# Two pairs' attention values together in eleven blocks, an opening in another order, and norm_g loaded by partitions (fp16 three-pass attention block, one core)

## The chip, the cores and the metric

The kernel runs on one core of one Trainium2 chip. The metric is the device time of one execution in microseconds (us). Before the change the median of three runs is 1378.2 us (1378.13 to 1381.88).

## The reference

One layer is computed on x of shape (1, 4096, 1024) in float32:

```
xn = rms_norm(x, norm_g)
q, k, v, z = split(xn @ w_in)          # 16 query heads, 4 key/value heads of 64
s = q k^T / 8 + bias[t5_bucket(distance)]   # keys of the last 128 positions only
p = softmax(concat(s, sink of the head))    # the sink's column is dropped afterwards
o = p v
x = x + (o * silu(z)) @ w_out
out = rms_norm(x, final_g)
```

All in float32. The kernel gets x as it is and a second time transposed, and the weights with their columns in an order that suits it.

## The kernel before

**Numbers.** TensorE works in fp16. Each operand is split into a high and a low fp16 half, and each product is three passes (high x high, high x low, low x high; PASSES, L331) that add up in one PSUM bank. A split takes two instructions: ScalarE writes the high half, and VectorE subtracts it from the operand and writes the low half (L161 to 163). Operands that are sums go through GpSimd first.

**Blocks and products.** The 4096 tokens are worked off in 16 blocks of 256 (counted 0 to 15 here; the change's own words count from one, so its "blocks 5 to 15" are 4 to 14). The projections to q and z and the output projection are 2 x 2 block products. In the first two or three blocks they are done plainly, with eight half-products; from then on with seven products of sums and differences, in a chain over three PSUM banks. Weight factors that don't stay in SBUF are streamed from DRAM (tag "ws").

**Attention in pairs.** A block has four pairs (gp, t): gp is a half of the key/value heads, t a half of the block's tokens. A pair goes through these steps, most of them twice (e = 0, 1, one key/value head each, with its four query heads):
- scores (L567 to 580): eight matmuls into a PSUM bank "s" (two buffers)
- post (L583 to 608, VectorE): bias, window and maximum
- exps (L612 to 617, ScalarE): exponentials with their sums
- normalise (L620 to 625, VectorE): the reciprocal of the sum (L623), then one multiplication of a 128 x 512 tile in SBUF (L625), "the norm"
- turn (L627 to 645): four transposes on TensorE into a PSUM bank "tp" (L634, two buffers); ScalarE writes the high half from it (L638), VectorE the low half (L641) and a masked copy (L642)
- values (L647 to 661): twelve matmuls of 128 x 64 weights with 512 columns into the PSUM bank "o"; two of them run side by side, each on its half of the array's columns
- gate (L666 to 668, VectorE): the product with silu(z), out of "o"

PSUM has eight banks: "tp" twice, "s" twice, "o", and "pa", "pb", "pc" for the products. A bank "tp" serves one more thing: the factors of the next block's rms_norm are turned into a row there by two transposes (x_row, L297), with which VectorE scales the transposed x (x_scale, L302) before it is split (x_split, L309 and L311). The first block uses a "tp" for its bias rows as well.

**The order.** Every block is 25 slots (SLOTS), and each product or half-product stands in one slot. A dict (STEADY, L848) says for each step in which slot, counted from its block's first, it stands. In "pairs" the twelve numbers of a pair are: scores, post, exps, norm and turn of e = 0, the same five of e = 1, then values and gate. Steps after slot 24 run beside the next block's: "slot 39" of one block is "slot 14" of the next. Within a slot the steps are put out by phase (PHASES, L785), in this order: bank, attn (post, values, gate, x_row), sum, norm, turn, high, move (x_scale), low, soft (exponentials), load, main (the product), scores. From slot 90 of the whole kernel on (STATIC), TensorE, ScalarE, VectorE and GpSimd each run their instructions in just that order. In the first 20 slots only TensorE's order is set by hand, between the two the scheduler orders them. The opening (L998), ahead of slot 0, is by hand on all four. SyncE issues the loads.

**The opening.** The first key and value weights are loaded (L110) behind x, transposed x and norm_g (L115, from ScalarE's queue); each of their eight parts is scaled by norm_g and split (split_kv, L995). Beside that the first block's x is squared, its factors are computed (x_factor, L282 and L284), turned (L297), x is scaled and split. Then the first projection (L463) runs.

Of the kernel before, what the change touches and what calls it, by code (L numbers as in the profile page):

```python
# [10 lines left out]
F16 = mybir.dt.float16  # L11
# [10 lines left out]
P = 128  # L22
KC = D // P
TB = 256
NTB = T // TB
# [33 lines left out]
def tile_swa_block(ctx, tc, x, xt, t5, norm_g, final_g, w_q, w_kv, w_z, sinks, w_out, hot, out):  # L59
    nc = tc.nc  # L60
# [3 lines left out]
    work = ctx.enter_context(tc.tile_pool(name="work", bufs=1))  # L64
# [9 lines left out]
    def atile(shape, dt, tag, bufs):  # L74
        return pools["attn"].tile(shape, dt, tag=tag, name=tag, bufs=bufs)
# [5 lines left out]
    def ps(tag, bufs=1, shape=(P, 512), dt=F32):  # L81
        return psum.tile(list(shape), dt, tag=tag, name=tag, bufs=bufs)


    gs = const.tile([P, KC], F32, name="gs")
    mhalf = const.tile([P, 1], F32, name="mhalf")
    nc.vector.memset(mhalf, -0.5)
# [13 lines left out]
    def load_xf(tb):  # L101

        for i in range(2):
            xf[tb, i] = work.tile([P, 4, TB], F32, tag="xf", name="xf", bufs=2)
            nc.sync.dma_start(xf[tb, i], xt[tb, :, 4 * i:4 * i + 4, :])

    def load_kv(kc):
        st = work.tile([P, 512], F32, tag=("q00", "q01", "q10", "q11", "z00", "z01", "z10", "z11")[kc], name="wst",
                       bufs=1)
        nc.sync.dma_start(st, w_kv[kc * P:(kc + 1) * P, :])  # L110
        return st

    load_xin(0)
    load_xf(0)
    nc.scalar.dma_start(gs, norm_g.rearrange("(c p) -> p c", p=P))  # L115
    kv = [load_kv(kc) for kc in range(KC)]
    th = const.tile([BUCKETS, H], F32, name="th")
    nc.scalar.dma_start(th, t5)
# [42 lines left out]
    def split(hi, lo, f, scale):  # L161
        nc.scalar.activation(hi, f, AF.Copy, scale=scale)
        nc.vector.scalar_tensor_tensor(lo, f, scale, hi, op0=OP.mult, op1=OP.subtract)
# [6 lines left out]
    def load_pair(w, c, st):  # L170

        for j in range(2):
            nc.sync.dma_start(st[:, j, :], w[(4 * j + c) * P:(4 * j + c + 1) * P, :])
        return st
# [24 lines left out]
    def plain_q(name, c, st):  # L199
        w = wq[HOME[name]]  # L200
        split(w[:, c, 0], w[:, c, 1], factor(name, True, st), g_of(name, True, c))
# [73 lines left out]
    def x_square(tb, t):  # L275

        sq[tb, t] = work.tile([P, 1], F32, tag="rs", name="rs", bufs=2)
        nc.scalar.activation(xin[tb, t], xin[tb, t], AF.Square, accum_out=sq[tb, t])
# [8 lines left out]
    def x_factor(tb):  # L287
        for t in range(2):
            xs[tb, t] = power(sq.pop((tb, t)), 1.0 / (D * SX * SX), EPS / (SX * SX), "x")

    rows = {}

    def x_row(tb):

        p = ps("tp", 2)[:, 0:TB]
        for t in range(2):
            nc.tensor.transpose(p[:, t * P:(t + 1) * P], xs[tb, t].to_broadcast([P, P]), ident)  # L297
        rows[tb] = p

    def x_scale(tb, i):  # L300
        f = xf[tb, i]
        nc.vector.tensor_tensor(f, f, rows[tb][:, None, :].to_broadcast([P, 4, TB]), op=OP.mult)  # L302
# [3 lines left out]
    def x_split(tb, i):  # L306

        d = work.tile([P, 4, 2, TB], F16, tag=f"xb{i}", name="xb", bufs=1)
        nc.scalar.activation(d[:, :, 0, :], xf[tb, i], AF.Copy)  # L309
        XB[tb, i] = d  # L310
        return lambda: nc.vector.tensor_tensor(d[:, :, 1, :], xf[tb, i], d[:, :, 0, :], op=OP.subtract)  # L311
# [121 lines left out]
    def shift_k(tb):  # L433

        keys_of.clear()
        nc.vector.tensor_copy(K[:, :, :, :, 0:P], K[:, :, :, :, TB:])
# [82 lines left out]
    gf = const.tile([P, D], F32, name="gf")  # L519

    def bias_rows():
        pe = ps("tp", 2)
        nc.tensor.matmul(pe[:H, :2 * WIN], th, hb, start=True, stop=True)
        return pe

# [23 lines left out]
    class Pair:  # L549


        def __init__(self, tb, gp, t):
            self.tb, self.gp, self.t = tb, gp, t
            self.first = tb == 0 and t == 0
            self.s, self.pt, self.pm, self.c = {}, {}, {}, None
            self.steps = [0, 0]

# [69 lines left out]
        def turn(self, e):  # L627

            self.step(e, 3)
            p = ps("tp", 2)  # L630
            pv = p.rearrange("p (h q) -> p h q", h=4)
            for u in range(4):
                r, hp = divmod(u, 2)
                nc.tensor.transpose(pv[:, 2 * hp:2 * hp + 2, r * HD:(r + 1) * HD], self.c[:, 4 * e + u, :P], ident)  # L634
            w = atile([P, 2, 512], F16, f"pt{e}", 1)
            m = atile([P, 2, 512], F16, f"pm{e}", 1)
            self.pt[e], self.pm[e] = w, m
            nc.scalar.activation(w[:, 0], p, AF.Copy, scale=SP)  # L638

            def low():  # L640
                nc.vector.scalar_tensor_tensor(w[:, 1], p, SP, w[:, 0], op0=OP.mult, op1=OP.subtract)  # L641
                nc.vector.tensor_tensor(m.rearrange("p l (h q) -> p (l h) q", h=4),  # L642
                                        w.rearrange("p l (h q) -> p (l h) q", h=4),
                                        own_m[:, None, :].to_broadcast([P, 8, P]), op=OP.mult)
            return low

        def values(self):  # L647

            o = ps("o")
            tb, t = self.tb, self.t  # L650
            if self.first:
                todo = [(self.pm, V[tb], 0)]
            else:
                todo = [(self.pt, V[tb] if t else V[tb - 1], 1 - t), (self.pm, DV[tb], t)]
            n = 3 * len(todo)
            k = 0
            for w, v, vt in todo:
                for vi, pi in PASSES:
                    for e in range(2):
                        g = 2 * self.gp + e  # L660
                        nc.tensor.matmul(o[e * HD:(e + 1) * HD, :], v[:, vt, vi, g * HD:(g + 1) * HD], w[e][:, pi],  # L661
                                         start=k == 0, stop=k == n - 1)
                    k += 1
            self.o = o
# [176 lines left out]
    def plain_t(slots, tb, key, names, left, place, done):  # L841
# [25 lines left out]
    }  # L867
    SHORT = (1, 2, 2, 4, 6, 2, 3, 3, 5, 7, 8, 9)

    def moved(pairs, by):  # L870
        return {p: tuple(s + d for s in v) for (p, v), d in zip(pairs.items(), by)}
# [7 lines left out]
    LAST = dict(STEADY, vd=LAST_V, dv=LAST_DV, zs12=LAST_Z12, zp22=LAST_ZP, zs22=LAST_Z22,  # L879
                pairs={p: tuple(s + d for d in SHORT) for p, s in zip(STEADY["pairs"], LAST_PAIRS)},  # L880
                oplain=LAST_O, yplain=dict(zip(BLOCKS, LAST_Y)), res=25)
# [2 lines left out]
    PLAIN_X = dict(xsplit=(21, 22), xsum={"t1": 22, "t2": 24, "t3": 26, "t4": 27},  # L884
                   xsumsplit={"t1": 23, "t2": 25, "t3": 29, "t4": 28})

    NEXT_TO_LAST = dict(STEADY, op=(49, 48, 47, 51), on=(50, 54), om=(51, 55), os=(52, 56))

    def block(tb):
        s0 = SLOTS * tb  # L890
        plan = {0: FIRST, NTB - 2: NEXT_TO_LAST, NTB - 1: LAST}.get(tb, STEADY)

# [5 lines left out]
        isplain = {n: tb < m for n, m in PLAIN.items()}  # L898
        last = tb == NTB - 1
        isplain["o"] |= last  # L900
        if tb in PAIRS_BY:
            plan = dict(plan, pairs=moved(plan["pairs"], PAIRS_BY[tb]))
        if isplain["z"]:
            plan = dict(plan, **PLAIN_X)
# [84 lines left out]
    for tb in range(NTB):  # L989
        block(tb)  # L990
# [4 lines left out]
    def split_kv(kc):  # L995
        split(wkv[:, kc, 0], wkv[:, kc, 1], kv[kc], gs[:, kc:kc + 1])

    def opening():  # L998
        shift_k(0)
        for t in range(2):  # L1000
            x_square(0, t)
        x_factor(0)
        split_kv(0)
        x_row(0)
        for i in range(2):
            x_scale(0, i)
        low = x_split(0, 0)
        split_kv(1)
        low()
        low = x_split(0, 1)  # L1010
        split_kv(2)
        low()
        rows = bias_rows()
        for kc in range(3, KC):
            split_kv(kc)
        first_kv()
        spread = make_bias(rows)
        for c in range(4):
            st = (work.tile([P, 2, D], F32, tag="ws", name="wst", bufs=4) if c < 3 else
                  ramp.tile([P, 2, D], F32, tag="raw3", name="wst", bufs=1))  # L1020
            raw["q", c] = load_pair(w_q, c, st)
        spread()
        for c in range(3):
            raw["z", c] = load_pair(w_z, c, ramp.tile([P, 2, D], F32, tag=f"raw{c}", name="wst", bufs=1))
        for name in BLOCKS[:2]:
            for c in range(4):
                plain_q(name, c, raw["q", c])
        low_k, low_v = evac_k(0, banks["k", 0]), evac_v(0, banks["v", 0])
        low_k()
        low_v()  # L1030
        for name in BLOCKS[2:]:
            for c in range(4):
                plain_q(name, c, raw["q", c])

    ENGINES = {mybir.EngineType.PE, mybir.EngineType.Activation, mybir.EngineType.DVE, mybir.EngineType.Pool}
    with tc.manual_schedule(engines=ENGINES):
        opening()
# [68 lines left out]
```

## Time and profile before

| | |
|---|---|
| median of three runs | 1378.2 us |
| profiled execution | 1378.95 us, span 1377.2 us |
| TensorE matmuls busy | 1338.4 us (97% of the span), granted clock 0.994 |
| VectorE busy | 1203.0 us (87%) |
| ScalarE busy | 799.8 us (58%) |
| GpSimd busy | 439.5 us (32%) |
| DMA | 381.65 MB, mean 277 GB/s |

The profile is one execution, recorded by the hardware profiler. PE is TensorE's matmuls, PEld its weight loads, DVE VectorE, ACT ScalarE, POOL GpSimd, SP SyncE. A row of a timeline gives the start in us, the duration in us, the engine, the line of the kernel, the operation and its tiles (out<-in); in brackets stands the idle time ahead of it and what ended it. A row of busy times by stretch gives the stretch, its length, then each engine's busy time with its count of instructions, the granted TensorE clock (1.00 is full speed), the busy share of the DMA engines and what they moved in GB/s. Matmuls are pipelined and their records overlap, so their own durations don't add up; distances from start to start do.

### The profile page before, as it was taken

The numbers are of one execution on the slowest core, as the hardware profiler recorded it, in microseconds if no ns is written. First come the engines' busy times: TensorE is split into PE (matmuls) and PEld (weight loads), VectorE is DVE, ScalarE is ACT, GpSimd is POOL, SyncE is SP. The second block draws the span as 40 slices with busy tenths as digits, with TensorE's granted clock in tenths as the row PEclk, the third lists the DMA queues.
The fourth block names the chain that finished last, engine by engine and source line by source line (L and its number), as shares of the span: only waits on it lengthen the run. The fifth ranks groups of instructions, "written<-read, shape, count | busy, mean of one in ns | idle before, by whom it ended". The sixth has DMA issues, their size and how long they took to land.

```text
span 1377.2 us, 39296 instructions
## 1 busy us (share of the span) xinstructions
PE 1338.4 (97%) x16246; PEld 1086.0 (79%) x16246; DVE 1203.0 (87%) x2719; ACT 799.8 (58%) x2052; POOL 439.5 (32%) x406
## 2 busy tenths in 40 slices
PE   5899999999999999999999999999999999999997
PEld 4898678687697888869788796978879697887963
DVE  6989898888879889898988989899898989989795
ACT  5767565655555665565565555566556555555562
POOL 0612333524324142341513224242322414333121
PEclk9899999999999999999999999999999999999999
DMA  9995996889978495876949677694966769486576
GB/s 356 316 386 216 342 388 225 335 325 345 353 264 333 175 340 192 288 268 231 346 148 334 225 267 265 235 339 150 336 243 242 285 219 337 166 323 225 198 266 260
DMA packets 75603, 381.65 MB, mean 277 GB/s; under 512 B 9472, under 2 KB 10784, under 8 KB 42912
## 3 DMA queue, kind: packets, MB, share of 16 engines
q1 hardware_dynamic: 64352, 358.12, 71.2%
q10 hardware_dynamic: 11072, 21.02, 4.1%
q8 instruction: 127, 2.08, 0.6%
q14 instruction: 52, 0.43, 0.1%
HBM read 340.05 MB, written 39.06 MB: 275 GB/s over the span
## 4 chain that ended last, share of the span: by engine, by line
PE 79%; DVE 10%; DMA 5%; issue 2%; ACT 2%; POOL 0%; SPq 0%; ACTq 0%; POOLq 0%; DVEq 0%
PE pa L375 16%; PE pb L375 16%; PE pc L704 10%; PE o L661 6%; PE pc L375 5%; PE s L580 5%; PE pb L394 5%; PE pc L473 5%; PE pa L704 5%; PE tp L634 3%; PE pb L704 3%; DVE wsp L239 2%; DMA wst<-in_wq 1%; DMA wst<-in_wz 1%; DVE c L608 1%
## 5 line engine op out<-in xcount | busy, mean ns | idle before, releaser
L375 PEld LDWEIGHTS <-ws 128*128 128x128 f16 x7008 | 401.1, 98 | 25.7 <-issue 14.1
L704 PEld LDWEIGHTS <-yo 128*128 128x128 f16 x1392 | 134.0, 98 | 145.5 <-issue 3.6
L375 PEld LDWEIGHTS <-wq 128*128 128x128 f16 x3984 | 227.1, 98 | 11.9 <-issue 6.5
L617 ACT ACTIVATE c<-c,m 128x129 f32<-128x129 f32 x512 | 199.2, 392 | 28.3 <-DVE m L608 27.6
L704 PE MATMUL pc<-ws,yo 128*128 128x512 f16 x744 | 170.4, 379 | 0.2 <-DMA ws<-wos 0.2
L608 DVE CUSTOM_DVE_ANT_0 c<-s,bias,sink 128x128 f32<-128x128 f32 x496 | 153.6, 348 | 7.3
L284 POOL TENSOR_TENSOR rr<-ms,mhalf 128x1 f32<-128x1 f32 x62 | 36.1, 589 | 343.2 <-DVE ms L282 275.7
L625 DVE TENSOR_TENSOR c<-c,rl 128x512 f32<-128x512 f32 x128 | 130.8, 1024 | 3.8
L641 DVE SCALAR_TENSOR_TENSOR pt<-tp,pt 128x512 f16<-128x512 f32 x128 | 87.2, 684 | 36.9 <-ACT pt L638 36.8
L375 PE MATMUL pb<-xs,ws 128*128 128x128 f16 x1872 | 111.2, 220 | 0.0
L322 POOL TENSOR_TENSOR xf<-xf 128x512 f32<-128x512 f32 x56 | 83.3, 1497 | 86.8 <-DVE xb L311 72.6
L580 PE MATMUL s<-K,q 128*128 128x192 f16 x1024 | 108.5, 247 | 2.1 <-DVE m L608 2.0
L698 DVE TENSOR_TENSOR yo<-y,yo 128x512 f16<-128x512 f32 x100 | 81.6, 816 | 32.5 <-ACT yo L697 32.5
L404 ACT ACTIVATE mc<-pa 128x512 f32<-128x512 f32 x67 | 39.9, 595 | 118.6 <-PE pa L375 92.5
L375 PE MATMUL pb<-xb,ws 128*128 128x128 f16 x1776 | 107.3, 221 | 0.0
L404 ACT ACTIVATE mc<-pb 128x512 f32<-128x512 f32 x53 | 31.6, 596 | 125.5 <-PE pb L375 93.2
L690 POOL TENSOR_TENSOR y<-y,y 128x512 f32<-128x512 f32 x48 | 75.7, 1576 | 88.4 <-DVE y L668 45.1
L642 DVE TENSOR_TENSOR pm<-pt,own_m 128x1024 f16<-128x1024 f16 x128 | 96.4, 755 | 3.7
L580 PEld LDWEIGHTS <-q 128*128 128x128 f16 x1024 | 86.2, 98 | 14.9 <-DVE m L608 3.6
L617 ACT ACTIVATION_READ_ACCUMULATOR c<-c,m 128x1 f32 x512 | 96.7, 189 | 0.0
L187 POOL TENSOR_TENSOR wst<-wst 128x512 f32<-128x512 f32 x48 | 71.1, 1491 | 79.4 <-ACT wst L225 45.6
L638 ACT ACTIVATE pt<-tp 128x512 f16<-128x512 f32 x128 | 74.1, 594 | 36.5 <-PE tp L634 28.7
(135 smaller groups left out, 2680.2 us busy)
## 6 DMA issues: line engine op xcount, KB each, us to landing
ws<-wos SPq DMA_DIRECT2D x68, 1024.0 KB, 5.4
ws<-wzss SPq DMA_DIRECT2D x52, 1024.0 KB, 5.5
ws<-wost SPq DMA_DIRECT2D x48, 1024.0 KB, 5.3
ws<-wzs SPq DMA_DIRECT2D x47, 1024.0 KB, 5.5
ws<-wqs SPq DMA_DIRECT2D x31, 1024.0 KB, 5.0
xin<-in_x SPq DMA_DIRECT2D x34, 512.0 KB, 4.3
xf<-in_xt SPq DMA_DIRECT2D x32, 512.0 KB, 4.4
r<-in_x SPq DMA_DIRECT2D x30, 512.0 KB, 5.3
```

The costliest lines, as they stand in the source:

```text
L322: nc.gpsimd.tensor_tensor(dst, l, r, op=OP.subtract)
L375: nc.tensor.matmul(place(p, c), left(kc, wi)[:, c * P:(c + 1) * P], right_x(tb, right, kc, xi), start=fresh and c == 0 and k == 0, stop=c ...
L580: nc.tensor.matmul(s[:, hp, 0:3 * HD], lhs, rhs, start=hl == 0, stop=hl == 1)
L608: nc.vector.tensor_tensor_reduce(out=cu, in0=sv, in1=b, scale=-1.0 / SCORE, scalar=sink[:, g, r, hp:hp + 1], op0=OP.add, op1=OP.min, accum ...
L617: nc.scalar.activation(cu, cu, AF.Exp, bias=self.m[:, u:u + 1], scale=-1.0, accum_out=self.l[:, u:u + 1])
L625: nc.vector.tensor_tensor(cu, cu, rl[:, :, None].to_broadcast([P, 4, P]), op=OP.mult)
L641: nc.vector.scalar_tensor_tensor(w[:, 1], p, SP, w[:, 0], op0=OP.mult, op1=OP.subtract)
L642: nc.vector.tensor_tensor(m.rearrange("p l (h q) -> p (l h) q", h=4), w.rearrange("p l (h q) -> p (l h) q", h=4), own_m[:, None, :].to_bro ...
L661: nc.tensor.matmul(o[e * HD:(e + 1) * HD, :], v[:, vt, vi, g * HD:(g + 1) * HD], w[e][:, pi], start=k == 0, stop=k == n - 1)
L690: nc.gpsimd.tensor_tensor(Y[(tb, *dst)], Y[(tb, *l)], Y[(tb, *r)], op=op)
L698: return lambda: nc.vector.tensor_tensor(yo[:, 1], s, yo[:, 0], op=OP.subtract)
L704: nc.tensor.matmul(p, YO[tb, left][:, yi, c * P:(c + 1) * P], right(c, wi), start=fresh and k == 0, stop=k == 11, skip_group_check=not fresh)
```

## The change

Four things are changed.
- In blocks 4 to 14 (MERGED) the values of pairs (0,t) and (1,t) stand in the same slot, 29 and 39, one after the other, and their gates in slots 30 and 40 (BY_TWO). Before, the four values stood in slots 25, 29, 36 and 39, the gates in 27, 31, 38 and 40. With that, the turn of (1,0), e = 1, goes from slot 26 to 25, that of (0,1), e = 1, from 32 to 31, and pair (1,1)'s two turns, both in slot 37 before, to slots 38 and 36, and its two norms, both in slot 35 before, to slots 35 and 34. The next block's row of factors goes from slot 13 to 14, and its scaling from slot 14 to 15.
- The two "tp" buffers become two banks "tp" and "tq". In the merged blocks the second pair's values go into "tq", and all turns and the row use "tp" alone; elsewhere turns alternate between the two (turn_bank). The second pair's turned tiles come out of buffers "wsp" and "op".
- In the opening, the first split of the key weights stands behind the row and the scaling of block 0's x.
- norm_g is handed over in the shape of its tile, (128, 8), and loaded as it lies in DRAM; before, it lay as 1024 numbers in a row and the load picked them one by one.

```
+    def turn_bank(tb):
+        turns.append(0)
+        return ps("tp" if MERGED <= tb < NTB - 1 or len(turns) % 2 else "tq")
...
-    nc.scalar.dma_start(gs, norm_g.rearrange("(c p) -> p c", p=P))
+    nc.scalar.dma_start(gs, norm_g)
...
-        p = ps("tp", 2)[:, 0:TB]
+        p = turn_bank(tb)[:, 0:TB]
...
+            self.second = MERGED <= tb < NTB - 1 and gp == 1
...
-            p = ps("tp", 2)
+            p = turn_bank(self.tb)
...
-            w = atile([P, 2, 512], F16, f"pt{e}", 1)
-            m = atile([P, 2, 512], F16, f"pm{e}", 1)
+            if self.second:
+                w = work.tile([P, 2, 512], F16, tag="wsp", name="pt", bufs=3)
+                m = work.tile([P, 2, 512], F16, tag="op" if self.pm else "wsp", name="pm", bufs=4 if self.pm else 3)
+            else:
+                w = atile([P, 2, 512], F16, f"pt{e}", 1)
+                m = atile([P, 2, 512], F16, f"pm{e}", 1)
...
-            o = ps("o")
+            o = ps("tq" if self.second else "o")
...
+    VA0, GA0, VA1, GA1, TN, TN1, T0, T1, XR, G1 = 29, 30, 39, 40, 35, 34, 38, 36, 14, 0
...
+    BY_TWO = {
+        "pairs": {(0, 0): (10, 11, 14, 20, 22, 12, 13, 17, 18, 20, VA0, GA0),
+                  (1, 0): (16, 17, 21, 22, 27, 18, 21, 23, 24, 25, VA0, GA0 + G1),
+                  (0, 1): (22, 23, 25, 26, 33, 24, 25, 28, 29, 31, VA1, GA1),
+                  (1, 1): (26, 28, 30, TN, T0, 29, 30, 33, TN1, T1, VA1, GA1 + G1)},
+        "xr": XR, "xscale": (XR + 1, XR + 1)}
...
+        if MERGED <= tb < NTB - 1:
+            plan = dict(plan, **BY_TWO)
...
         x_factor(0)
-        split_kv(0)
         x_row(0)
         for i in range(2):
             x_scale(0, i)
+        split_kv(0)
         low = x_split(0, 0)
...
-    for n in ("t5_table", "norm_g", "final_g"):
-        give(f"in_{n}", rows(inputs[n]).reshape(-1) if n != "t5_table" else rows(inputs[n]))
+    give("in_t5_table", rows(inputs["t5_table"]))
+    give("in_norm_g", rows(inputs["norm_g"]).reshape(KC, P).T)
+    give("in_final_g", rows(inputs["final_g"]).reshape(-1))
```

For comparison, the pairs of the plan before:

```
        "pairs": {(0, 0): (10, 11, 14, 20, 22, 12, 13, 17, 18, 20, 25, 27),
                  (1, 0): (16, 17, 21, 22, 27, 18, 21, 23, 24, 26, 29, 31),
                  (0, 1): (22, 23, 25, 26, 33, 24, 25, 28, 29, 32, 36, 38),
                  (1, 1): (26, 28, 30, 35, 37, 29, 30, 33, 35, 37, 39, 40)},
        "xr": 13, "xscale": (14, 14),
```

More of the change, by code (lines that the diff above doesn't have):

```diff
@@ L82, in ps @@
         return psum.tile(list(shape), dt, tag=tag, name=tag, bufs=bufs)
+    MERGED = 4
+    turns = []
+    def turn_bank(tb):
+        turns.append(0)
+        return ps("tp" if MERGED <= tb < NTB - 1 or len(turns) % 2 else "tq")
     gs = const.tile([P, KC], F32, name="gs")
@@ L521, in bias_rows @@
     def bias_rows():
-        pe = ps("tp", 2)
+        pe = turn_bank(0)
         nc.tensor.matmul(pe[:H, :2 * WIN], th, hb, start=True, stop=True)
```

## The prediction

> **What bounds the kernel now.** The head of the page gives the span.
>
> ```profile
> span 1377.2 us, 39296 instructions
> ```
>
> The profiled execution took 1378.95 us around a span of 1377.2 us (the 1.75 us lie outside the span), 0.75 us above the median of 1378.2 us. First I read busy time by stretch, with one steady block (block 5) and a stretch of another.
>
> ```profile
> core 0: us, PE busy (x) PEld busy (x) DVE busy (x) ACT busy (x) POOL busy (x), PEclk, DMA share, GB/s
> 425.74:506.97 81.23, 81.23 (x1000) 66.43 (x999) 72.66 (x164) 46.74 (x124) 26.12 (x25) 1.00 0.72 260
> 737.48:765.69 28.21, 28.21 (x281) 19.78 (x279) 27.70 (x59) 17.27 (x46) 12.38 (x10) 1.00 0.95 350
> ```
>
> TensorE is busy for all 81.23 us of the block at full clock: it never waits, and what it saves or waits here is the kernel's time. The second row is slots 15 to 24 of one block: VectorE is busy 27.70 of 28.21 us there, so it is a second bound in that half of the block, and it runs behind TensorE. Next, TensorE's timeline of that block.
>
> ```profile
> 720.00 0.82 PE L580 MATMUL s<-K,q 128*128 128x192 f16 x8
> 720.76 0.84 PE L661 MATMUL o<-pt,v 128*64 128x512 f16 x6
> 721.43 0.81 PE L661 MATMUL o<-pm,dv 128*64 128x512 f16 x6
> 722.18 2.85 PE L375 MATMUL pb<-xb,ws 128*128 128x128 f16 x48
> ...
> 744.83 2.75 PE L704 MATMUL pc<-ws,yo 128*128 128x512 f16 x12
> 747.42 0.82 PE L580 MATMUL s<-K,q 128*128 128x192 f16 x8
> 748.08 2.75 PE L704 MATMUL pa<-ws,yo 128*128 128x512 f16 x12
> 750.67 0.60 PE L634 MATMUL tp<-ident,c 128*128 128x128 f32 x4
> ...
> 756.37 0.60 PE L634 MATMUL tp<-ident,c 128*128 128x128 f32 x4
> ...
> 765.24 0.82 PE L580 MATMUL s<-K,q 128*128 128x192 f16 x8
> ```
>
> Matmuls overlap, so I count from start to start. Two turns of pair (0,0) start at 750.67 (slot 20) and 756.37 (slot 22); at 765.24 come the scores that end slot 24. Now VectorE in the same stretch.
>
> ```profile
> 731.80 2.35 DVE L302 TENSOR_TENSOR xf<-xf,tp 128x1024 f32<-128x1024 f32 x2
> 734.06 0.69 DVE L668 SCALAR_TENSOR_TENSOR y<-o,z 128x512 f32<-128x512 f32 x1
> 737.48 0.69 DVE L698 TENSOR_TENSOR yo<-y,yo 128x512 f16<-128x512 f32 x1 [2.73 <-ACT yo L697]
> ...
> 756.13 0.68 DVE L641 SCALAR_TENSOR_TENSOR pt<-tp,pt 128x512 f16<-128x512 f32 x1
> ...
> 765.69 1.78 DVE L625 TENSOR_TENSOR c<-c,rl 128x512 f32<-128x512 f32 x1
> ```
>
> At 737.48 VectorE has been idle 2.73 us for ScalarE's yo, which ScalarE makes after it has emptied slot 14's product: here VectorE is in step with TensorE. From there it runs without a pause, and is a slot or more behind by slot 20.
>
> **Part 1: two pairs' values together (eleven blocks).** What it removes: a group of values costs more than its matmuls. Eight score matmuls before an ordinary product take 748.08 - 747.42 = 0.66 us, and before values 720.76 - 720.00 = 0.76: 0.10 to enter. Twelve 512-column matmuls take 747.42 - 744.83 = 2.59 us, 0.216 each; values run two halves of the columns side by side, so twelve are six steps, 1.295 us, where 722.18 - 720.76 = 1.42 are spent: 0.125 to leave. Together 0.225 us a group. Four groups in a block become two: 0.45 us a block, 5.0 us in eleven. The moved turns and the row of factors keep their 0.44 and 0.22 us.
>
> What it adds is waits. The two "tp" buffers become one, since "tq" now holds the second pair's values. The turn in slot 22 must then wait until L641 has read slot 20's turn: it ends at 756.13 + 0.68 = 756.81, and TensorE starts 0.05 us after its releaser (as at 15.01 below, after work that ended at 13.90 + 1.06 = 14.96). The turn stood at 756.37, so it waits 0.49 us, with every later matmul behind it.
>
> The larger wait is at slot 25. Pair (1,0)'s first turn moves from slot 26 to 25, and the values that stood ahead of slot 25's product are gone, so TensorE reaches the turn when the scores of slot 24 are issued, at 765.24 + 0.66 = 765.90. It needs what the norm of slot 24 (L625) writes. That is VectorE's row at 765.69, which ends at 767.47. The turn waits until 767.52, 1.62 us, and the first wait lies within it, as the norm's time is VectorE's own: 1.62 us in all, not 2.11. This holds if slots 15 to 24 run as before, and the plan changes nothing in them on any engine from slot 15's "low" phase on. Two things are moved ahead of that point, the scaling of x (2.35 us at 731.80) to slot 15 and a gate (0.69 us) to the same slot. Values and row end at about 733.2, the second gate then 733.9, the scaling 736.2, before the 737.48 at which VectorE starts again: the 2.73 us of idle time cover them. If they did not, VectorE would be later still, and the wait longer.
>
> The turn of slot 27 needs L641 of slot 25's turn. In VectorE's order that stands ahead of the norm of slot 26 now, and by my count it is done before TensorE arrives; I take 0 there, with 0.4 us as the other end. The turns of the other two pairs (slots 31 and 33, 36 and 38) fall where VectorE is in step, and I count nothing. The values of pair (1,1), one slot after their last turn, have about 1 us to spare. Net: 1.62 - 0.45 = +1.17 us a block, 12.9 us in eleven.
>
> What decides 1.62 is a contest that the next rows show.
>
> ```profile
> 765.65 1.27 POOL L719 TENSOR_TENSOR r<-r,mc 128x512 f32<-128x512 f32 x1 [1.02 <-DVE rl L623]
> ```
> ```profile
> L625 DVE TENSOR_TENSOR c<-c,rl x4: 692/1773/1778, 745.1 to 765.7; 128x512 f32<-128x512 f32 x4
> ```
>
> Four norms of this stretch take 0.69 us at the least and 1.77 in the middle; the one at 765.69 begins 0.04 us after an addition on GpSimd and takes the long time. If it came first, it would end at 766.38, and the turn would wait 0.53 us. Both are released by VectorE's own work just before, so I keep 1.62 (0.53 is the lower end). The Trainium skill's "SBUF — State Buffer", section "Who interferes with whom", says that a VectorE instruction with two SBUF inputs and a GpSimd instruction that reads SBUF exclude each other for a whole instruction and that issue order decides who blocks; by that rule the short case is as real as the long one, and the trace has both lengths.
>
> Does a wait lower the clock? One of this length stands in block 15.
>
> ```profile
> 1320.43 0.59 PE L661 MATMUL o<-pt,v 128*64 128x512 f16 x3 [1.69 <-DVE pt L641]
> ```
> ```profile
> 1320.00:1324.00 4.00, 3.46 (x19) 1.49 (x19) 3.86 (x15) 1.69 (x8) 0.00 (x0) 1.00 0.46 195
> ```
>
> After 1.69 us the granted clock stays 1.00. I count nothing, and let the upper end hold some, as here the waits come in every block.
>
> **Part 2: the opening.**
>
> ```profile
> 8.78 0.47 PE L297 MATMUL tp<-ident,rr 128*128 128x128 f32 x1 [1.21 <-POOL rr L284]
> ```
> ```profile
> 15.01 0.37 PE L463 MATMUL pa<-xb,wkv 128*128 128x256 f16 x1 [4.79 <-ACT xb L309]
> ```
> ```profile
> 11.23 0.72 ACT L162 ACTIVATE wkv<-wst,gs 128x512 f16<-128x512 f32 x1 [3.32 <-DMA wst<-in_wkv]
> 13.90 1.06 ACT L309 ACTIVATE xb<-xf 128x1024 f16<-128x1024 f32 x1 [1.95 <-DVE xf L302]
> ```
> ```profile
> 11.98 0.75 DVE L163 SCALAR_TENSOR_TENSOR wkv<-wst,gs,wkv 128x512 f16<-128x512 f32 x1 [3.89 <-ACT wkv L162]
> 12.65 2.35 DVE L302 TENSOR_TENSOR xf<-xf,tp 128x1024 f32<-128x1024 f32 x2
> ```
> ```profile
> DMA to landing us min/median/max: 6.5/7.4/8.4
> ```
> ```profile
> 30.55 1.21 ACT L444 ACTIVATE K<-pa 64x512 f16<-64x512 f32 x2 [2.03 <-PE pa L463]
> ```
> ```profile
> 40.00:50.00 10.00, 10.00 (x183) 10.00 (x180) 9.94 (x12) 9.90 (x18) 7.31 (x6) 1.00 0.78 249
> ```
> ```profile
> 58.83 3.38 PE L375 MATMUL pa<-xb,ws 128*128 128x128 f16 x30 [2.85 <-DVE ws L163]
> ```
>
> The scaling stood behind the split of the first key weights, which land at 11.2. Its factors are there at 8.78 + 0.47 = 9.25, and x lands 6.5 and 8.4 us after its issues at about 1.6 and 2.1, near 8.1 and 10.5. Scaled first, the halves are done at 10.5 and 11.7; ScalarE goes from the weights (11.95) straight to xb, and TensorE starts at 13.06, not 15.01: 1.95 us. The rest of the chain keeps its order and shifts as much. ScalarE's 2.03 us of idle time before 30.55, for the projection's end, are the room into which it passes on; then ScalarE and VectorE are busy throughout (9.90 and 9.94 of 10 us) and TensorE waits for them at 58.83, so 1.95 us arrive there, and behind it TensorE is the bound. Cover: were the splits late for their loads instead, nothing would arrive.
>
> **Part 3: norm_g by partitions.**
>
> ```profile
> SPq L110 <- DMA gs<-in_norm_g: 3.1, 1, 3.1
> ```
> ```profile
> 3.00:4.00 1.00, 0.00 (x0) 0.00 (x0) 0.00 (x0) 0.00 (x0) 0.00 (x0) 1.00 0.97 208
> ```
>
> SyncE's first weight load waits 3.1 us for norm_g, which comes as 1024 single numbers; meanwhile the DMA engines are 0.97 busy at 208 GB/s, where 0.95 gave 350 above. At 350 this microsecond would have moved 0.14 MB more, 0.4 us of transfer. In one run of eight numbers for each partition most of that should go, and the weights behind it land so much earlier. I take 0.4 us, between 0 (x goes ahead of it in the queue) and 0.8 (the wait holds further such microseconds). A loss has no row: the same bytes come in fewer pieces. Opening: -2.3 us, from 0 to -2.8.
>
> **Sum.** 1378.95 + 12.9 - 2.3 = 1389.5 for a profiled execution; as medians stand 0.75 lower, 1388.8 us. From the bounds (opening 0 to -2.8, 0.4 us more a block, a lowered clock now and then) this case reaches from 1385 to 1395.
>
> **The rivals.** *No new wait, only the saving*: if VectorE came to the two places in time, 5.0 and 2.3 us go and the kernel takes 1370.9 us. For it: TensorE has no slack anywhere, so any saving counts, and the moved gate and scaling leave VectorE's second half untouched. Against: rows 756.13 and 765.69 against 756.37 and 765.90. It decides if VectorE is 1.6 us earlier at slot 24 than before. Chance 0.20. *The norm goes first*: the wait is 0.53 us, a block costs 0.08 more, and with the opening the kernel takes 1376.8 us. For it: a 0.04 us margin at 765.65; against: it has to fall so in every block. With cases in which the long wait comes in a few blocks only, 0.15. *The single bank alone*: the Trainium skill's "Perfetto Trace Analysis", section "Optimizing Tensor Performance", asks that matmul groups rotate through PSUM banks so that emptying one overlaps the next, which "tp" no longer does. As a mechanism here it is the 0.49 us of slot 22, 0.04 more than the saving, again 1376.3 us; it is inside the 0.15. The forecast has 0.65; nothing speaks for the edit not doing what it says.
>
> **How the numbers follow.** A change of 0.3% (4.1 us) is about what can be told from none here. Slower by more: the forecast, 0.65. Within: 0.15. Faster by more: 0.20. The range has to reach into the faster case to leave out no more than 2 in 10: 1371 to 1395; the forecast's own is 1385 to 1395.
>
> **What would show it.** Right: a steady block of about 82.4 us instead of 81.23; TensorE's waits list "tp L634" for VectorE's c L625 some eleven times at 1.1 to 1.6 us, and for pt L641 at 0.5; entering and leaving values twice a block; the first projection matmul near 13 us. Wrong: a block under 81.2, or no wait at the turns; then the step that VectorE's order keeps its times has failed. If the first projection starts earlier and 58.83 does not move, Part 2's carry has failed.

## The result

The changed kernel takes 1392.6 us in the median (1390.6 to 1396.5, 6 runs), the kernel before 1378.4 us: a ratio of 1.010 (95% interval 1.0083 to 1.0118), slower by 14.2 us where 10.6 were forecast. The profiled execution took 1393.45 us.

In the changed kernel the lines have moved down: the turn's transposes are L644 (before: L634), VectorE's readings of the turn L655 and L656 (L641, L642), the norm L635 (L625), the values L675 (L661), the output product L718 (L704), the split of yo L712 (L698), the addition out of PSUM L729 (L715), GpSimd's addition L733 (L719). First the head of the page, then a steady block and slots 15 to 24 of block 8, in the columns that the prediction used.

```profile
span 1391.7 us, 39247 instructions
```
```profile
547.72:630.27 82.55, 81.21 (x1001) 66.61 (x999) 73.10 (x164) 46.80 (x125) 26.17 (x24) 1.00 0.70 256
741.08:769.31 28.23, 27.90 (x275) 19.26 (x273) 27.71 (x60) 16.99 (x45) 12.06 (x10) 1.00 0.94 344
```

A block takes 82.55 us instead of 81.23, and TensorE, which never paused, now stands still for 1.34 us of it. VectorE's stretch is the same within 0.02 us: 27.71 us of work in 28.23, against 27.70 in 28.21. What TensorE waits for, over the whole execution (total, times, longest):

```profile
PE tp L644 <- DVE c L635: 11.1, 11, 1.0
...
PE tp L644 <- DVE pt L655: 3.7, 11, 0.3
```

Both new waits are there, once in each of the eleven blocks. Here is TensorE's timeline of block 8, then VectorE's and GpSimd's.

```profile
754.27 0.60 PE L644 MATMUL tp<-ident,c 128*128 128x128 f32 x4
760.48 0.66 PE L644 MATMUL tp<-ident,c 128*128 128x128 f32 x4 [0.33 <-DVE pt L655]
763.56 0.82 PE L590 MATMUL s<-K,q 128*128 128x192 f16 x8
769.40 0.82 PE L590 MATMUL s<-K,q 128*128 128x192 f16 x8
771.23 0.63 PE L644 MATMUL tp<-ident,c 128*128 128x128 f32 x4 [1.01 <-DVE c L635]
```
```profile
741.08 0.69 DVE L712 TENSOR_TENSOR yo<-y,yo 128x512 f16<-128x512 f32 x1 [1.24 <-ACT yo L711]
...
759.74 0.68 DVE L655 SCALAR_TENSOR_TENSOR pt<-tp,pt 128x512 f16<-128x512 f32 x1
...
768.50 0.69 DVE L729 SCALAR_TENSOR_TENSOR r<-pb,r 128x512 f32<-128x512 f32 x1
769.10 0.17 DVE L633 RECIPROCAL rl<-l 128x4 f32<-128x4 f32 x1
769.31 1.78 DVE L635 TENSOR_TENSOR c<-c,rl 128x512 f32<-128x512 f32 x1
771.01 1.75 DVE L712 TENSOR_TENSOR yo<-y,yo 128x512 f16<-128x512 f32 x1
```
```profile
769.27 1.27 POOL L733 TENSOR_TENSOR r<-r,mc 128x512 f32<-128x512 f32 x1 [1.03 <-DVE rl L633]
770.49 3.40 POOL L331 TENSOR_TENSOR xf<-xf 128x512 f32<-128x512 f32 x2
```

The brackets count only the time after the earlier matmuls' modelled ends; from start to start the waits are longer. Slots 20 and 22 lay 756.37 - 750.67 = 5.70 us apart before and lie 760.48 - 754.27 = 6.21 apart now: 0.51 us, for the reading that ends at 759.74 + 0.68 = 760.42. At slot 25 TensorE arrives at 769.40 + 0.66 = 770.06, the norm ends at 771.09, and the turn starts at 771.23: 1.17 us. GpSimd's addition has again started 0.04 us ahead of the norm, and the norm takes 1.78 us. The yo behind it meets GpSimd's next addition (row 770.49) and takes 1.75 us, where the yo at 741.08 takes 0.69.

The end of the kernel shows one difference that the edits don't explain: after a wait that both kernels have, the clock falls only in the changed one.

```profile
1333.24 0.59 PE L675 MATMUL o<-pt,v 128*64 128x512 f16 x3 [1.69 <-DVE pt L655]
1333.48 1.29 PE L675 MATMUL o<-pm,dv 128*64 128x512 f16 x6
1334.70 4.45 PE L718 MATMUL pa<-ws,yo 128*128 128x512 f16 x12
1338.99 0.82 PE L590 MATMUL s<-K,q 128*128 128x192 f16 x8
```
```profile
1333.00:1336.00 3.00, 2.66 (x13) 0.97 (x13) 2.86 (x14) 1.40 (x7) 0.00 (x0) 0.79 0.51 213
1336.00:1339.00 3.00, 3.00 (x11) 1.15 (x10) 2.27 (x4) 0.30 (x2) 1.78 (x2) 0.64 0.00 0
```

The product after it takes 1338.99 - 1334.70 = 4.29 us; from 1335 to 1338 us the granted clock is 0.50. In the experiment with the new values alone (below) the same wait, 1.69 us long, is followed by a product of 2.76 us. Of the thirteen profiled executions of this study, the kernel before among them, three show the slow product there, and one of the three is a version of the kernel before. It is a draw of some 1.7 us, and none of the change's doing. The traces of both kernels hold more such falls to 0.50: each has one behind the last waits of the opening, between 54 and 65 us, and one behind TensorE's wait near 144 us.

### The profile page after: what moved, and what is told of

It is laid out like the page before. It is cut to its first block, busy times and chain, and to the rows that moved or that the text cites. A ratio compares the mean times of both kernels' runs of the same rounds, so it can differ in the third digit from the quotient of the medians.

```text
span 1391.7 us, 39247 instructions
## 1 busy us (share of the span) xinstructions
PE 1339.3 (96%) x16246; PEld 1088.1 (78%) x16246; DVE 1206.7 (87%) x2719; ACT 801.2 (58%) x2052; POOL 439.1 (32%) x406
## 4 chain that ended last, share of the span: by engine, by line
PE 55%; DVE 27%; issue 4%; DMA 2%; ACT 2%; POOL 0%; POOLq 0%; SPq 0%; DVEq 0%; ACTq 0%
PE pa L384 13%; PE pb L384 11%; PE pb L403 5%; PE pc L482 5%; PE pc L718 4%; DVE c L618 4%; PE o L675 4%; DVE c L635 3%; PE pc L384 3%; PE s L590 3%; DVE xb L320 3%; PE tp L644 3%; DVE yo L712 2%; DVE wsp L248 2%; PE tq L675 2%
## 5 line engine op out<-in xcount | busy, mean ns | idle before, releaser
L718 PEld LDWEIGHTS <-yo 128*128 128x128 f16 x1392 | 134.5, 98 | 145.8 <-issue 4.8
L718 PE MATMUL pc<-ws,yo 128*128 128x512 f16 x744 | 170.4, 379 | 0.0
L652 ACT ACTIVATE pt<-tp 128x512 f16<-128x512 f32 x108 | 64.3, 595 | 138.2 <-PE tp L644 135.0
L635 DVE TENSOR_TENSOR c<-c,rl 128x512 f32<-128x512 f32 x128 | 130.7, 1023 | 3.8
L704 POOL TENSOR_TENSOR y<-y,y 128x512 f32<-128x512 f32 x48 | 75.8, 1579 | 95.8 <-DVE y L682 54.5
L656 DVE TENSOR_TENSOR pm<-pt,own_m 128x1024 f16<-128x1024 f16 x128 | 96.2, 753 | 3.7
L712 DVE TENSOR_TENSOR yo<-y,yo 128x512 f16<-128x512 f32 x100 | 80.7, 808 | 16.1 <-ACT yo L711 16.0
L718 PE MATMUL pa<-ws,yo 128*128 128x512 f16 x384 | 89.8, 384 | 0.0
L609 DVE COPY_PREDICATED s<-sel,s 128x128 f32<-128x128 int32 x256 | 73.2, 290 | 17.2 <-PE s L590 16.7
```

Of the source, the lines that this page charges most:

```text
L609: nc.vector.copy_predicated(dst, sel[:, None, :].to_broadcast([P, 2, HD]), src)
L635: nc.vector.tensor_tensor(cu, cu, rl[:, :, None].to_broadcast([P, 4, P]), op=OP.mult)
L704: nc.gpsimd.tensor_tensor(Y[(tb, *dst)], Y[(tb, *l)], Y[(tb, *r)], op=op)
L712: return lambda: nc.vector.tensor_tensor(yo[:, 1], s, yo[:, 0], op=OP.subtract)
L718: nc.tensor.matmul(p, YO[tb, left][:, yi, c * P:(c + 1) * P], right(c, wi), start=fresh and k == 0, stop=k == 11, skip_group_check=not fresh)
```

## The experiments

The theory: the loss lies in the eleven merged blocks. With one bank for all turns, and a turn put close behind its norm, TensorE now comes to two places before VectorE, which runs a slot or more late there; the longer of the two waits is as long as it is because the norm takes more than twice its time beside GpSimd's addition. The rivals: that the new opening or the other buffers cost; that a single bank costs in any order; that a turn moved ahead of its norm is the whole of it. The ratios are against runs of the kernel before on the same chip, whose medians were 1378.3 to 1379.7 us; so ratios compare across experiments, medians only roughly. "Block" is the distance between the starts of two blocks' key projections in the steady part.

| kernel | block, us | median, us | ratio to before (95% interval) |
|---|---|---|---|
| before | 81.23 | 1378.4 | |
| changed | 82.55 | 1392.6 | 1.010 (1.0083 to 1.0118) |
| values alone | 82.53 | 1394.0 | 1.0117 (1.0102 to 1.0132) |
| opening alone | 81.23 | 1378.1 | 0.9996 (0.9983 to 1.0008) |
| opening alone, again | 81.23 | 1377.1 | 0.9979 (0.9970 to 0.9988) |
| norm_g alone | 81.23 | 1378.1 | 0.9996 (0.9985 to 1.0006) |
| turns exchanged | 81.75 | 1385.2 | 1.0051 (1.0032 to 1.0069) |
| turns spread | 81.80 | 1386.0 | 1.0055 (1.0038 to 1.0072) |
| first turn in slot 26 | 83.14 | 1398.1 | 1.0137 (1.0122 to 1.0152) |
| norm first | 81.35 | 1379.1 | 0.9996 (0.9987 to 1.0005) |
| before, norm first | 81.23 | 1379.7 | 0.9996 (0.9986 to 1.0006) |
| early norms | 80.80 | 1374.9 | 0.9967 (0.9954 to 0.9980) |
| early norms, old opening | 80.80 | 1374.5 | 0.9962 (0.9950 to 0.9975) |

**The two halves of the change by themselves.** The values alone are the changed kernel with this undone:

```
-    nc.scalar.dma_start(gs, norm_g)
+    nc.scalar.dma_start(gs, norm_g.rearrange("(c p) -> p c", p=P))
...
         x_factor(0)
+        split_kv(0)
         x_row(0)
         for i in range(2):
             x_scale(0, i)
-        split_kv(0)
```

> The changed kernel with the opening and norm_g as before: the merged values and the single bank alone. Theory (the loss is in the eleven merged blocks, two waits at the turns of slots 22 and 25 against two saved groups of values): a steady block takes 82.55 us as in the changed kernel, TensorE's first projection starts at 15.0 us, and the time is about 1394.5 us, some 2 us above the changed kernel's 1392.6. Rival (the new opening disturbs what follows and costs part of the 14 us): 1388 us or less.

It took 1394.0 us with the same block within 0.02 us and the same two waits (the norm's again 11.1 us in eleven). So the loss is the values', and the new opening cost nothing of it. The opening alone puts that same edit into the kernel before:

> The kernel before with the new opening and the new norm_g alone. Theory: the first projection starts at 12.8 us, the steady block stays at 81.23 us, and 1.5 to 2.6 us are gained: 1376 to 1377 us. Rival (the saving is taken back before the first merged block): 1378.4 us. Rival (the opening costs): 1380 us or more.

Its first projection started at 13.24 us, but the median was only 0.1 us below, with an interval from -2.3 to +1.1 us. It was run again:

> The kernel before with the new opening and norm_g, as tried already, in more rounds. Theory (the 2.5 us that reach TensorE's last wait of the opening, near 58 us, go on to the end): a ratio near 0.998, 2 to 2.5 us. Rival (they are taken back in blocks 0 to 3, where TensorE still waits for VectorE now and then): a ratio within 0.001 of 1.

This time 0.9979, a gain of 1.7 to 4.1 us. The two intervals meet near 2 us, what the forecast had. Two more pairs of kernels differ by the opening alone: the values alone against the changed kernel, 1.4 us, and the two with early norms, which showed nothing. Where it goes can be followed part of the way. TensorE's last wait of the opening ends at 56.1 us on the average of eight profiled executions with both edits (55.6 to 56.8) and at 58.5 in four without (58.0 to 58.9), a gain of 2.4 us. At block 4's key projection it is 1.1 us (383.1 against 384.1), but there the executions with both edits lie up to 3.4 us apart. So part of the gain seems to be taken back in blocks 0 to 3, and how much reaches the end is not settled. norm_g by itself:

> The kernel before with norm_g by partitions alone. Theory (norm_g's load holds the weights' first load back by 3.1 us, but the first projection waits for x's scaling behind it): the wait of SyncE's queue falls below 1 us, the first projection starts up to 0.6 us earlier than at 15.0, and the time stays within 1 us of 1378.3. Rival (all of the opening's gain is norm_g's): the projection starts near 13.2 us as with both edits.

SyncE's queue still waited 2.1 us for it (2.6 to 3.1 in the four profiled executions without the edit; below 1 had been expected). The projection started at 14.44 us, against 15.0 to 15.4 in those four and 12.4 to 13.3 with both edits, so the scaling's place is the larger part of the opening, as expected. The ratio cannot be told from 1. This execution reached block 4 at 381.5 us, sooner than seven of the eight with both edits: what stands at block 4 in single executions says little about the opening.

**Which turn stands behind which norm.** Pair (1,0)'s two turns exchanged:

```
-                  (1, 0): (16, 17, 21, 22, 27, 18, 21, 23, 24, 25, VA0, GA0 + G1),
+                  (1, 0): (16, 17, 21, 22, 25, 18, 21, 23, 24, 27, VA0, GA0 + G1),
```

> The changed kernel with pair (1,0)'s two turns exchanged: e = 0, whose norm is two slots older, in slot 25, and e = 1 in slot 27. Theory (slot 25's wait of 1.17 us is for the norm of slot 24): that wait is gone; TensorE then comes to slot 27's turn at 1.17 us less, 0.28 us ahead of VectorE's reading of the bank, so 0.3 us come back; block 81.66 us, in all 1382.8 us. Rival (what costs is one bank for all turns, in whatever order): the wait stays near 1 us, 1390 us or more.

TensorE's timeline of block 8, and what VectorE did for slot 27:

```profile
757.81 0.66 PE L644 MATMUL tp<-ident,c 128*128 128x128 f32 x4 [0.30 <-DVE pt L655]
760.89 0.82 PE L590 MATMUL s<-K,q 128*128 128x192 f16 x8
766.73 0.82 PE L590 MATMUL s<-K,q 128*128 128x192 f16 x8
767.39 0.60 PE L644 MATMUL tp<-ident,c 128*128 128x128 f32 x4
773.18 0.91 PE L590 MATMUL s<-K,q 128*128 128x192 f16 x8
774.19 0.66 PE L644 MATMUL tp<-ident,c 128*128 128x128 f32 x4
```
```profile
773.45 0.69 DVE L655 SCALAR_TENSOR_TENSOR pt<-tp,pt 128x512 f16<-128x512 f32 x1
```

The turn of slot 25 follows its scores by 0.66 us, without a wait. At slot 27 TensorE would have been there at 773.18 + 0.66 = 773.84 and starts at 774.19, when the bank has been read: 0.35 us come back, 0.28 had been worked out. The block is 81.75 us (expected 81.66).

The other way round, the first turn put back to slot 26, where the kernel before had it:

```
-                  (1, 0): (16, 17, 21, 22, 27, 18, 21, 23, 24, 25, VA0, GA0 + G1),
+                  (1, 0): (16, 17, 21, 22, 27, 18, 21, 23, 24, 26, VA0, GA0 + G1),
```

> The changed kernel with pair (1,0)'s first turn back in slot 26, where it stood before the change. Theory (one bank: the turn in slot 27 has to wait for VectorE's reading of this one, which comes near 778.3 us on the changed kernel's time axis where TensorE arrives at 776.5): slot 25's wait goes and one of about 1.9 us comes at slot 27; block 83.3 us, in all 1400 us, slower still. Rival (the loss is that the turn was moved ahead of its norm, and goes with the move): 81.4 us a block, 1380 us.

```profile
776.02 0.61 PE L644 MATMUL tp<-ident,c 128*128 128x128 f32 x4
779.14 0.88 PE L590 MATMUL s<-K,q 128*128 128x192 f16 x8
781.54 0.66 PE L644 MATMUL tp<-ident,c 128*128 128x128 f32 x4 [1.51 <-DVE pt L655]
```

The norm is no longer waited for, and slot 27 waits 781.54 - 779.80 = 1.74 us for the bank: 83.14 us a block, the slowest of all. The move to slot 25 was not what cost; with one bank it was the better of the two places.

**The norm and GpSimd's addition.** Both come right behind VectorE's work out of PSUM at 768.50 (L729). In this kernel the norm goes ahead of that work, with its exponentials one slot earlier on ScalarE, and nothing else changes in VectorE's or GpSimd's order in these blocks:

```
-                  (1, 0): (16, 17, 21, 22, 27, 18, 21, 23, 24, 25, VA0, GA0 + G1),
+                  (1, 0): (16, 17, 21, 22, 27, 18, 21, 22, 23, 25, VA0, GA0 + G1),
```

> The changed kernel with one thing moved: on VectorE the norm of pair (1,0), e = 1, stands ahead of the addition out of PSUM that it followed (its exponentials one slot earlier with it), so that GpSimd's addition, which waits for that one, cannot start beside the norm. Theory (the norm takes 1.78 us because GpSimd starts 0.04 us ahead of it): the norm takes 0.69 us and ends before TensorE comes, slot 25's wait of 1.17 us is gone, slot 22's 0.51 stays: block 81.38 us, in all 1379.7 us. Rival (the length of the norm is not GpSimd's doing, or VectorE is late anyway): the norm stays near 1.78 us or the wait above 0.8, 1388 us or more.

TensorE, VectorE and GpSimd in block 8:

```profile
764.99 0.82 PE L590 MATMUL s<-K,q 128*128 128x192 f16 x8
765.65 0.60 PE L644 MATMUL tp<-ident,c 128*128 128x128 f32 x4
```
```profile
764.30 0.69 DVE L635 TENSOR_TENSOR c<-c,rl 128x512 f32<-128x512 f32 x1
764.91 0.68 DVE L729 SCALAR_TENSOR_TENSOR r<-pb,r 128x512 f32<-128x512 f32 x1
765.51 0.68 DVE L712 TENSOR_TENSOR yo<-y,yo 128x512 f16<-128x512 f32 x1
```
```profile
765.67 1.64 POOL L733 TENSOR_TENSOR r<-r,mc 128x512 f32<-128x512 f32 x1 [1.84 <-DVE r L729]
```

The norm takes 0.69 us and the turn no longer waits; now VectorE's yo is first by 0.16 us and takes 0.68 us, where it took 1.75 in the changed kernel, and GpSimd's addition takes 1.64 us instead of 1.27. So this order takes 2.2 us from VectorE's work in a block (73.10 to 70.91), the norm and the yo about half each. The block is 81.35 us, and the time that of the kernel before. The same edit in the kernel before is the counter-check:

> The kernel before with the norm of pair (1,0), e = 1, ahead of the addition on VectorE, as in the changed kernel with the norm first. Theory (a norm of 0.69 instead of 1.78 us is worth time only where TensorE comes before it has ended): the norm gets short, the steady block stays at 81.23 us, and the time stays within 1 us of the kernel before. Rival (VectorE's contention with GpSimd slows the kernel by itself): up to 1.1 us a block, 1366 to 1372 us.

```profile
765.46 0.69 DVE L625 TENSOR_TENSOR c<-c,rl 128x512 f32<-128x512 f32 x1
```

The norm is as short, the block stays at 81.23 us, and the time stays, though VectorE is busy 17.7 us less over the whole execution (1185.3 against 1203.0): the long norm was there before the change, and cost nothing as long as TensorE did not come to wait.

**A version without waits.** A first try spread the turns and moved no norm:

```
-        "pairs": {(0, 0): (10, 11, 14, 20, 22, 12, 13, 17, 18, 20, VA0, GA0),
-                  (1, 0): (16, 17, 21, 22, 27, 18, 21, 23, 24, 25, VA0, GA0 + G1),
+        "pairs": {(0, 0): (10, 11, 14, 20, 22, 12, 13, 17, 18, 19, VA0, GA0),
+                  (1, 0): (16, 17, 21, 22, 24, 18, 21, 23, 24, 27, VA0, GA0 + G1),
```

> As the swap, with the turns spread out: (0,0) e = 1 in slot 19 instead of 20, (1,0) e = 0 in slot 24 and e = 1 in 27. Theory: VectorE then reads each turn ahead of the next one although there is a single bank; neither wait is left, only the saving of 0.40 us a block: block 80.83 us, in all 1373.7 us, faster than both kernels. Rival (one bank for the turns always costs; VectorE is late wherever they stand): waits of 0.3 to 1 us a block are left, 1377 to 1388 us.

```profile
758.82 0.63 PE L644 MATMUL tp<-ident,c 128*128 128x128 f32 x4 [0.30 <-DVE c L635]
...
774.97 0.50 PE L590 MATMUL s<-K,q 128*128 128x192 f16 x4 [0.31 <-DVE m L618]
```

That was a miss, the rival was right: no turn waits for the bank, but slot 22's waits for the norm of slot 20, and the scores of slot 26 wait for VectorE's post, behind which the earlier readings had been put. A reading that is moved ahead moves something else back. So VectorE itself had to get done sooner, with the norm of slot 20 one slot earlier and the norm of slot 24 out of GpSimd's way:

```
-        "pairs": {(0, 0): (10, 11, 14, 20, 22, 12, 13, 17, 18, 20, VA0, GA0),
-                  (1, 0): (16, 17, 21, 22, 27, 18, 21, 23, 24, 25, VA0, GA0 + G1),
+        "pairs": {(0, 0): (10, 11, 14, 19, 22, 12, 13, 17, 18, 19, VA0, GA0),
+                  (1, 0): (16, 17, 21, 22, 25, 18, 21, 22, 23, 27, VA0, GA0 + G1),
```

> The exchange of the two turns of (1,0), the norm first, and pair (0,0)'s norm and first turn in slot 19 instead of 20. Theory (what costs is VectorE's lateness at the turns, and with each norm and each reading of the bank ahead of its turn a single bank is enough): no wait at the turns of slots 19, 22, 25 and 27, block 80.83 us, in all 1373.7 us, faster than both kernels. Rival (VectorE has no room left in this half of the block, the lateness only moves to slots 26 and 27): waits of 0.3 to 0.8 us a block, 81.1 to 81.6 us, 1377 to 1382 us.

```profile
546.60:627.40 80.80, 80.80 (x1001) 66.69 (x999) 69.38 (x164) 46.81 (x125) 24.77 (x24) 1.00 0.72 262
```

TensorE is busy without a gap again, in a block of 80.80 us. VectorE does the 164 instructions of the changed kernel's block in 69.38 us instead of 73.10. In the groups by line, the norms, yo, xs (L338) and xb (L320), the last two low halves of splits, take 1.1 us less each, and pm 0.7 us more. This version takes 1374.9 us, 0.9967 of the kernel before: faster than both. With the old opening:

> The version with the early norms, with the opening and norm_g as before the change. Theory (the merged values alone save 0.43 us in each of eleven blocks once no turn waits): block 80.80 us, in all 4 to 5 us under the kernel before, 1374 us where that takes 1378.5. Rival (the 4 us came mostly from the opening): 1377 us or more.

1374.5 us (0.9962): its gain is the merged values'.

## Why the prediction was right

**The place and the mechanism.** The two waits stand where they were put, for the instructions named, once in each of eleven blocks; VectorE's run from slot 15 to 24 kept its length, on which the sum rested. The first wait was 0.51 us (forecast 0.49), both together 0.51 + 1.17 = 1.68 by the starts of the turns (1.62), and the first lay within the forecast's 1.62 as it had argued.

**The saving** was forecast as 0.45 us a block, and the kernel with early norms, which has no wait left, measures it: 81.23 - 80.80 = 0.43. (No run has the order with early norms and the values as before; but TensorE has no gap in either block, so the difference is TensorE's own work.)

**The mis-sized term** is the waits' price. Between 80.80 and 82.55 us lie 1.75 us, of which 1.68 are seen in the starts; two turns that take 0.66 and 0.63 instead of 0.60 us, as rows 760.48 and 771.23 show, are about the size of the rest. At slot 25 the turn started 0.14 us behind the norm's end (771.23 against 771.09), where 0.05 had been counted. Slot 27's turn did not wait, as counted. A block lost 82.55 - 81.23 = 1.32 us instead of 1.17, in eleven 14.5 instead of 12.9.

**The opening.** The first projection began at 12.77 us (forecast 13.06 by Part 2 alone, 12.7 with Part 3's 0.4 us), and TensorE's last wait ended 2.8 us earlier in the profiled pair (forecast 2.3), as Part 2 had it. "Behind it TensorE is the bound" was too simple: it still waits here and there in blocks 0 to 3, and at block 4's key projection the profiled pair was 1.7 us apart. In Part 3, norm_g's wait fell from 3.1 us to 1.7 only. By the medians, the opening's forecast is not confirmed: the two kernels lie 14.2 us apart (11.4 to 16.3 by the interval), and the blocks alone make 14.5.

**The clock.** It was counted at nothing, and it took 1.7 us near the end of the profiled execution, in a place that both kernels have. The forecast rested on one wait of 1.69 us that had left the clock at 1.00; the same trace holds a fall to 0.50 for about 3.4 us behind waits of 1.28 and 0.77 us at 144 and 145 us. So one row could not show that a wait is safe. The new waits in the merged blocks themselves never lowered it, as forecast. The profiled sum comes out so: 0.6 us less from the opening than forecast, 1.6 more in the eleven blocks and 1.7 from the clock make the 3.9 us by which 1393.45 lies above 1389.5. That the sum closes is no proof of its parts, since single executions differ by as much.

**The rivals.** "No new wait, only the saving" was wrong for this change, but the version with early norms shows that it is what the edit is worth where VectorE is in time: 1374.9 us, where 1370.9 had been worked out with the whole of the opening. "The norm goes first" didn't fall so by itself in any block; made to, it gave 1379.1 us (1376.8 worked out), with the 0.51 us of slot 22 left, as that case had said. The rule of the Trainium skill that stood behind it, that VectorE with two SBUF inputs and GpSimd reading SBUF exclude each other and that issue order decides who blocks ("SBUF — State Buffer", section "Who interferes with whom"), agrees with all of these rows: 1.78 us for the norm when GpSimd was first, 0.69 with no GpSimd addition beside it, and 1.64 for the addition when VectorE's yo was first. The single bank alone cost 0.5 us a block in this order, and nothing in the order with early norms.

## What to carry to other kernels

Where one engine is busy without a gap, ask of every instruction that is moved ahead or loses a buffer not what it costs but when its inputs are ready, on the timeline of the engine that makes them: here 0.43 us a block were won and 1.75 lost, though no instruction was added. An engine that is only 87% busy over the kernel can be full in one part of a block, and there the order of its work counts as well as the length. A contention that costs nothing today (the long norm) becomes the price when the slack behind it is spent; moving one instruction past its neighbour took it away.

## What the runs showed of the hardware

- The same wait of 1.67 to 1.69 us on TensorE, at the same place, was followed by a slower clock in three of thirteen profiled executions and left it at 1.00 in the others; where it fell, it was 0.50 for about 3.4 us, and the product of 2.76 us took 4.00 to 4.45 us. Behind the wait near 144 us it fell in nine of the thirteen. Waits of 1.01 us (the changed kernel) and 1.51 us (first turn in slot 26), once in each of eleven blocks, never lowered it. The Trainium skill's "TensorE: Matmul & The Clock Gate", section "Part 1: The HAM clock gate (the "warmup" mystery)", says that the activity window is free-running, so that the number of slow matmuls at a kernel's start differs from run to run; a fall that comes in some executions only agrees with that. It names an idle window of about 3.4 us for the fall, and here the clock fell behind a wait of 1.69 us.
- Two orders of the same 164 instructions kept VectorE busy for 73.10 and for 69.38 us of a block. Where rows show the reason (the norm and the yo), it is an addition on GpSimd beside them: 1.75 to 1.78 us with it, 0.68 to 0.69 without or when VectorE was first. In the kernel before, 17.7 us less of VectorE's work over the execution left the time as it was (ratio 0.9996).
